# A two-layer hybrid model block in float32 on one core: written first steps, one-shape scores among a projection's matmuls, a second place for two weights, and partition swaps on ACT

## The chip, the core and the metric

The kernel runs on one core of a Trainium2 chip. The core has a matrix engine (TensorE, in the profile PE for matmuls and PEld for weight loads), a vector engine (DVE), a scalar engine (ACT), GpSimd (POOL) and a queue engine (SP) from which most transfers are issued. The metric is the device time of one execution in microseconds (us), as the median of several runs.

## The reference, cut to what matters

Two layers over 256 tokens of width 1024. Each layer has a mixer and a gated feed-forward part, and each of these is preceded by a normalization that is scaled and shifted by a conditioning vector c. Layer 0's mixer is a gated linear recurrence in chunks; layer 1's is attention with three branches (compressed blocks, selected blocks, window).

```python
c_act = silu(c)
mods = einsum('bd,lde->lbe', c_act, ada_w) + ada_b      # shift, scale, gate of 4 sublayers
# layer 0
h = rms_norm(x, gain) * (1 + scale) + shift
q, f, i, g = split(h @ w_in)          # 4 x 1024 columns
q = silu(q); log_f = log_sigmoid(f); k = 1 - exp(log_f)
# per head, with G = cumsum(log_f):
attn[t, s] = sum_d q[t, d] * k[s, d] * exp(G[t, d] - G[s, d])     # s <= t
o = rms_norm(attn @ i + state terms) * silu(g)
x = x + gate * (o @ w_out);  x = x + gate * swiglu(h')
# layer 1
k_cmp, v_cmp, k_sel, v_sel, k_win, v_win = split(modulate(x, kv_norm) @ w_kv)
kc = rms_norm(silu(blocks(k_cmp) @ w1) @ w2)       # compressed keys, values alike
q = rms_norm(h @ w_q); k_sel, k_win = rope(rms_norm(.)); q_rope = rope(q)
o = g0 * attend(q, kc, vc) + g1 * attend(q_rope, k_sel, v_sel) + g2 * attend(q_rope, k_win, v_win)
x = x + gate * (o @ w_out);  x = x + gate * swiglu(h'')
```

## The kernel before, in words

Activations lie transposed: width on 128 partitions in eight chunks, 256 tokens along the free dimension. Products are made nearly float32 in three matmuls (`mm3`, L484): each weight and each activation is split into a rounded part and a residual, `wh`, `wl` and `hh`, `hl`. ACT makes `wh` by a cast (L309) and DVE makes `wl` by a subtraction (L310), two halves of 128x1024 for each weight chunk.

**The stream of weights.** All weights come as chunks of 128x2048 float32 (1 MB) in one list, SCHED, whose order is written by hand through ORDER. `issue` (L284) starts transfers from SP into a ring of RAW = 4 buffers; `process` (L293) takes the next chunk and either splits it ("lin"), holds it as it is ("raw": the compression's four weight chunks w1, of which each step c0 and c1 uses two), or uses it for conditioning. A held chunk keeps its buffer until `release_raw` (L336); `issue` lets the list run at most RAW chunks past the oldest held one. Conditioning chunks are reduced on DVE (`ada`, L354: two reductions over 1024 columns and small operations) or multiplied on PE (`ada_pe`, L376) with a 32-column stationary operand.

**Order of the instructions.** A program step is written in sequence, and the tile framework then places the instructions of each engine by their readiness and priority, so a later step's matmuls may come ahead of an earlier step's. `issue_after` ties an instruction behind a given one; `after` (L435) adds an order without a wait.

**Start.** `build` loads crow (c as a row), x in two halves, the columns and the first ring. It spreads c over the partitions (`crep`, L249, two matmuls and Silu on ACT). `first_stat` (L553) squares x (two quarters on ACT, two on DVE), adds the quarters in three DVE operations of 512 columns (L567), and sums over partitions and the remaining two chunks with two fp32 matmuls (`ms`, L569, each recorded as two passes). Then comes the inverse root: Ln and Exp on ACT, and four DVE operations (L574 to L578).

**Recurrent layer** (`hgrn`, L674). For each of the eight input chunks k: one conditioning chunk on DVE, `full_chunk` (L599: t on DVE, hh on ACT, hl on DVE), and 48 matmuls with the q and f columns. Then ORDER["hgrn"] is walked: D makes the decays X of two pairs of heads (ACT exponentials, DVE products; a pool of 14 X buffers), i and g are projections of 48 matmuls, S and T are the scores of a pair of heads, V the values. A pair has four calls of `head_scores` (L862): 24 small matmuls into psl, and the "upper" scores into psu: one matmul with 64 columns (L880) and two with 32 (L884). T differs from S in that projection g2 is cut into eight pieces (`gate_steps`, L724) and tied between the calls.

**Attention layer** (`nsa`, L1019). It projects keys and values (kv), makes hq (the queries' normalized input, `full_pair` L608) and hk (the values'), then walks ORDER["nsa"]: c compression (two halves), q query projections, G gates, n query norms, s, x, v scores and values, w the value projection, a conditioning. hh and hl of "which 0" share the memory h0; the k and v compression projections read it, and hk is written into it ahead of the compression. `rotate` (L983) makes the rotary embedding; it needs each group of 32 partitions exchanged with its neighbour, and does that with four transfers of 64 KB issued from ACT (L989). It is called for two key tiles and four query tiles.

## Time and profile before

| | |
|---|---|
| runs of the kernel | 749.25, 749.32, 747.56 us; median 749.25 |
| the profiled execution | span 749.9 us from its first to its last instruction; no other time of it is given |
| PE busy | 719.1 us (96%) |
| DVE busy | 587.9 us (78%) |
| ACT busy | 410.8 us (55%) |
| moved from HBM | 170.48 MB, 229 GB/s over the span |

A row of a timeline holds the start, the duration, the engine, the line of the kernel, the operation, the tiles written and read, their shapes and the count; in brackets stand the idle time of the engine before it and what ended that. A group row holds the count, the busy time of the group and the mean of one in ns, then the idle time before them. PE's busy time includes waiting inside the pipeline, so the distance between starts of matmuls says more than the busy share. A matmul in float32 is recorded as two passes.

### The profile page before, as it was taken

Reading aid. Unit: us, or ns where it says so; the run is one execution under the profiler, and the core shown is the slowest. Engines: PE = TensorE matmul, PEld = TensorE weight load, DVE = VectorE, ACT = ScalarE, POOL = GpSimd, SP = SyncE. Lnnn points to the kernel's source line nnn. Section 1 sums busy time; section 2 is a strip of 40 time slices with the busy share of each in tenths; the row PEclk is TensorE's granted clock in tenths of the full one; section 3 lists DMA queues with packets and bytes.
Section 4 is the critical chain, followed back from the end, with each engine's and each line's share of the span. In section 5 each row is a group of like instructions: output and inputs, shape, how many; then the busy total and the mean of one; then the engine's idle time right before and its main releaser. Section 6 shows DMA issues by size and latency. Waiting matters only on the chain.

```text
span 749.9 us, 14669 instructions
## 1 busy us (share of the span) xinstructions
PE 719.1 (96%) x5892; PEld 634.2 (85%) x5892; DVE 587.9 (78%) x1221; ACT 410.8 (55%) x796; POOL 0.4 (0%) x5
## 2 busy tenths in 40 slices
PE   4999998899999999999999789999999999999997
PEld 2999986799999999988897688655799888888886
DVE  6995988479898988898689667777689869776642
ACT  4348868356645544544476443756666665565330
POOL 0000000000000000000000000000000000000000
PEclk9999999999999999999999998999999999999999
DMA  8998737556389797888733834355764555756710
GB/s 343 340 346 343 272 111 276 208 222 225 120 338 385 273 362 272 328 317 319 283 113 96 318 121 141 113 196 198 282 212 181 193 201 214 268 191 225 271 45 21
DMA packets 26566, 174.05 MB, mean 232 GB/s; under 512 B 3201, under 2 KB 4609, under 8 KB 6018
## 3 DMA queue, kind: packets, MB, share of 16 engines
q1 hardware_dynamic: 24912, 170.80, 61.1%
q10 hardware_dynamic: 1586, 2.32, 1.1%
q8 instruction: 46, 0.75, 0.4%
q14 instruction: 22, 0.18, 0.1%
HBM read 170.48 MB, written 1.05 MB: 229 GB/s over the span
## 4 chain that ended last, share of the span: by engine, by line
PE 86%; DVE 7%; DMA 3%; ACT 2%; issue 1%; ACTq 0%; DVEq 0%
PE ffo L498 11%; PE ff L486 6%; PE ff L488 6%; PE ff L487 6%; PE ffo L499 6%; PE ff L498 5%; PE ff L499 2%; PE adapsss L387 2%; PE po L1321 2%; DMA usq<-huq 2%; PE ptt L1304 2%; DVE wl L310 2%; PE s L1264 1%; PE q L487 1%; PE hg_i L781 1%; PE hg_g L486 1%
## 5 line engine op out<-in xcount | busy, mean ns | idle before, releaser
L309 ACT CAST wh<-raw 128x1024 fp32r<-128x1024 f32 x201 | 208.9, 1048 | 170.3 <-PE ffo L498 47.7
L310 DVE TENSOR_TENSOR wl<-raw,wh 128x1024 fp32r<-128x1024 f32 x201 | 244.2, 1221 | 58.5 <-ACT wh L309 57.8
L498 PE MATMUL ffo<-g,wh 128*128 128x512 f32 x352 | 123.5, 394 | 0.0
L499 PE MATMUL ffo<-g,wl 128*128 128x256 f32 x352 | 99.1, 282 | 0.0
L486 PE MATMUL ff<-hh,wh 128*128 128x256 f32 (+1 forms) x352 | 99.0, 282 | 0.0
L487 PE MATMUL ff<-hl,wh 128*128 128x256 f32 (+1 forms) x352 | 98.9, 282 | 0.0
L488 PE MATMUL ff<-hh,wl 128*128 128x256 f32 (+1 forms) x352 | 98.7, 281 | 0.0
L498 PEld LDWEIGHTS ffo<-g,wh 128*128 128x128 f32 x352 | 66.2, 188 | 15.3
L361 DVE CUSTOM_DVE_ANT_0 junk<-raw,crep 128x1024 f32<-128x1024 f32 x64 | 78.1, 1220 | 0.5
L488 PEld LDWEIGHTS ff<-hh,wl 128*128 128x128 f32 x352 | 66.5, 189 | 0.0
L487 PEld LDWEIGHTS ff<-hl,wh 128*128 128x128 f32 x352 | 66.3, 189 | 0.2
L486 PEld LDWEIGHTS ff<-hh,wh 128*128 128x128 f32 x352 | 66.2, 188 | 0.0
L499 PEld LDWEIGHTS ffo<-g,wl 128*128 128x128 f32 x352 | 66.1, 188 | 0.0
L498 PE MATMUL ff<-h,wh 128*128 128x512 f32 x152 | 54.2, 395 | 0.0
L499 PE MATMUL ff<-h,wl 128*128 128x256 f32 x152 | 42.6, 280 | 0.0
L498 PEld LDWEIGHTS ff<-h,wh 128*128 128x128 f32 x152 | 28.7, 189 | 6.8 <-DVE h L605 0.2
L431 ACT ACTIVATE Pt<-Pt,nm 128x128 f32<-128x128 f32 x64 | 28.1, 442 | 8.9 <-DVE nm L1273 8.8
L656 DVE SCALAR_TENSOR_TENSOR x<-ffo,mod,x 128x256 f32<-128x256 f32 x32 | 15.4, 482 | 18.4 <-PE ffo L499 18.1
L499 PEld LDWEIGHTS ff<-h,wl 128*128 128x128 f32 x152 | 28.6, 188 | 0.0
L481 ACT CAST g<-fg 128x256 fp32r<-128x256 f32 x44 | 17.8, 404 | 17.4 <-DVE fg L950 16.5
L488 PE MATMUL nq<-hh,wl 128*128 128x256 f32 x64 | 20.1, 314 | 3.6 <-DVE wl L310 3.6
L1269 DVE CUSTOM_DVE_ANT_0 Pt<-s,cst 128x128 f32<-128x128 f32 (+1 forms) x64 | 19.1, 352 | 2.8 <-PE s L1264 2.7
(453 smaller groups left out, 1741.4 us busy)
## 6 DMA issues: line engine op xcount, KB each, us to landing
raw<-in_w SPq DMA_DIRECT2D x160, 1024.0 KB, 5.3
x<-in_x SPq DMA_DIRECT2D x2, 512.0 KB, 4.8
usq<-huq ACTq DMA_DIRECT2D x16, 64.0 KB, 2.1
out<-x SPq DMA_DIRECT2D x8, 128.0 KB, 1.9
cst<-in_cst ACTq DMA_DIRECT2D x1, 558.0 KB, 6.9
usk<-huk ACTq DMA_DIRECT2D x8, 64.0 KB, 2.8
raw<-in_w SPq DMA_DIRECT2D x1, 512.0 KB
rselr<-in_rsel SPq DMA_DIRECT2D x1, 256.0 KB, 2.7
```

The source lines that it names most:

```text
L309: nc.scalar.copy(wh, u)
L310: nc.vector.tensor_tensor(wl, u, wh.bitcast(F32), op=ALU.subtract)
L361: nc.vector.tensor_tensor_reduce(out=junk, in0=t[:, h * D:(h + 1) * D], in1=self.crep, scale=1.0, scalar=0.0, op0=ALU.mult, op1=ALU.add, a ...
L431: r = nc.scalar.activation(out, in_, func, **kw)
L481: self.nc.scalar.copy(hi, v)
L486: mm(ps, lhsT=wh, rhs=hh, start=first, stop=False)
L487: mm(ps, lhsT=wh, rhs=hl, start=False, stop=False)
L488: return mm(ps, lhsT=wl, rhs=hh, start=False, stop=last)
L498: mm(ps, lhsT=w[k][0], rhs=b, start=k == 0, stop=False)
L499: mm(ps[:, 0], lhsT=w[k][1], rhs=b[:, 0], start=False, stop=k == n - 1)
L656: nc.vector.scalar_tensor_tensor(xn[:, m], p, gate[:, m:m + 1], xn[:, m], op0=ALU.mult, op1=ALU.add)
L1269: nc.vector.tensor_tensor_reduce(out=Pt[half][:, br, o:o + n], in0=ps[half][:, br], in1=cs[:, S - n:], scale=1.0, scalar=-3e38, op0=ALU.ad ...
```

## The change

1. **First steps.** `startup` replaces the steps of `build` and most of `first_stat`. Each half of x gets its own run: a square on ACT, a square on DVE, two additions on DVE, one `ms` matmul. `chain` adds an order without a wait to the instructions of ACT, of DVE and of PE, in which the Silu of c stands between the squares. For layer 0 the small steps of a conditioning chunk go to ACT, with a product `gb` made once. The inverse root has two operations on DVE (L574 to L578 had four), with a Square and a product on ACT, and the first conditioning chunk is processed ahead of them. Chunks 1 to 7 use `first_chunk`: x times the normalizer on DVE, scale and shift on ACT, a copy on ACT, a subtraction on DVE.
2. **Filler.** 14 matmuls of zeros (bf16, 256 columns) stand between the mean and the first projection.
3. **Scores.** The 64-column matmul of the upper scores becomes two of 32 columns. Projection g1 is cut into four pieces that are tied between the calls of S0; g2 is cut into eight over S2 and S3 as before; conditioning chunks of layer 0's gate and of sublayer 1 move to other places in the list ("hada").
4. **A second home.** The chunks w1 2 and 3 (LATE) no longer use the ring. `load_late` puts them into the memory of h0 after the k projections; hk is made after the compression (step K behind c1); `issue` counts held buffers; and chunks up to nq0 are processed right after `load_late`.
5. **Swaps.** The four transfers of `rotate` become four copies on ACT.

```diff
 ORDER = {
-        "D0 i0 g0 S1 i1 S0 V0 D1 g1 i2 i3 T2 T3 V1"
+        "D0 i0 g0 S1 i1 g1/4 S0 c1 V0 D1 i2 i3 g2/8 S2 S3 V1 g3"
-    "hada": [1, 1, 3, 4, 6, 6, 6, 7, 7, 7, 8, 8],
+    "hada": [1, 1, 2, 2, 3, 3, 4, 4, 7, 7, 8, 8],
-        "c0 q0 c1 G q1 n0 x0 s0 w0 q2 s1 q3 w1 s2 v0 v1 ...
+        "c0 q0 c1 K G q1 n0 x0 s0 w0 q2 s1 q3 w1 s2 v0 v1 ...
+LATE = [("raw", "w1", 2), ("raw", "w1", 3)]
     def issue(self, n):
-        n = min(n, len(SCHED), min(self.held, default=n) + RAW)
+        n = min(n, len(SCHED))
+        free = RAW - sum(i < self.n_proc for i in self.held)
+        ring = [i for i in range(self.n_proc, n) if SCHED[i] not in LATE]
+        n = min(n, ring[free]) if len(ring) > free else n
         while self.n_dma < n:
+            if SCHED[self.n_dma] in LATE:
+                self.n_dma += 1
+                continue
...
+    def load_late(self):
+        t = self.hp.tile([P, KD, 2, 258], F32R, tag="h0", name="w1late").rearrange("p k e s -> p (k e s)").bitcast(F32)
+        for kind in range(2):
+            n = SCHED.index(LATE[kind])
+            d = t[:, kind * CH:(kind + 1) * CH]
+            self.nc.sync.dma_start(d, self.a["w"][n])
+            self.rawready[("w1", 2 + kind)] = (None, d)
...
-        if kind == "ada_ss":
+        if kind == "ada_ss" and l == 0:
+            nc.scalar.activation(A[:, i:i + 1], m[:, c1:c1 + 1], AF.Identity, scale=gain[:, i:i + 1],
+                                 bias=self.gb[:, i:i + 1])
+            nc.scalar.activation(m[:, i:i + 1], m[:, i:i + 1], AF.Identity, bias=bias[:, i:i + 1])
...
+    def startup(self, crow):
+        v.memset(mean, 1.0 / D)
...
+        pe = [nc.tensor.matmul(p, lhsT=self.ones[0:1, :], rhs=crow[0:1, 512 * h:512 * h + 512], start=True, stop=True)
+              for h, p in enumerate(pc)]
+        on_act, on_dve = [], []
+        for h in range(2):
+            c, d = 4 * h, 4 * h + 2
+            on_act.append(nc.scalar.activation(sq[:, c:d], x[:, c:d], AF.Square))
+            on_act.append(self.act(self.crep[:, 512 * h:512 * h + 512], pc[h], AF.Silu))
+            on_dve += [v.tensor_tensor(sq[:, d:d + 2], x[:, d:d + 2], x[:, d:d + 2], op=ALU.mult),
+                       v.tensor_tensor(sq[:, c:d], sq[:, c:d], sq[:, d:d + 2], op=ALU.add),
+                       v.tensor_tensor(sq[:, c], sq[:, c], sq[:, c + 1], op=ALU.add)]
+            pe.append(nc.tensor.matmul(ps, lhsT=mean, rhs=sq[:, c], start=h == 0, stop=h == 1))
+        on_act.append(self.act(cc, self.col("c"), AF.Silu))
+        self.chain(*on_act)
+        self.chain(*pe)
+        self.warm = pe[-1]
+        on_dve.append(v.tensor_scalar_add(self.b1, self.cols[:, lo:lo + 112], 1.0))
+        on_dve.append(v.tensor_tensor(self.gb, self.b1[:, 8:16], self.col(self.gain(0)), op=ALU.mult))
+        on_dve.append(v.tensor_copy(self.c32, cc[:, :, None].to_broadcast([P, 8, 32])))
+        self.chain(*on_dve)
     def first_stat(self):
         self.act(y, ps, AF.Ln, bias=self.eps)
         self.act(y, y, AF.Exp, scale=-0.5)
-        nc.vector.tensor_tensor(t, y, y, op=ALU.mult)
+        nc.scalar.activation(t, y, AF.Square)
+        nc.scalar.mul(w, y, -0.5)
+        self.process()
         nc.vector.scalar_tensor_tensor(t, ps, EPS, t, op0=ALU.add, op1=ALU.mult)
-        nc.vector.tensor_scalar(t, t, -0.5, 1.5, op0=ALU.mult, op1=ALU.add)
-        nc.vector.tensor_tensor(self.rstd, t, y, op=ALU.mult)
+        nc.vector.scalar_tensor_tensor(self.rstd, t, -3.0, w, op0=ALU.add, op1=ALU.mult)
+    def first_chunk(self, hh, hl, m, A, sh, pool):
+        r = nc.vector.tensor_tensor(xr, self.x[:, m], self.rstd, op=ALU.mult)
+        self.after(r, self.hl_prev)
+        nc.scalar.activation(t, xr, AF.Identity, scale=A[:, m:m + 1], bias=sh[:, m:m + 1])
+        self.last_hh = nc.scalar.copy(hh[:, m, :256], t)
+        self.hl_prev = nc.vector.tensor_tensor(hl[:, m, :256], t, hh[:, m, :256].bitcast(F32), op=ALU.subtract)
...
+            for _ in range(14):
+                z = nc.tensor.matmul(pq[0][:, 0], lhsT=self.zero, rhs=self.zero[:, :1].to_broadcast([P, S]), start=True, stop=True)
+                self.after(z, self.warm)
+                self.warm = z
...
-        nc.tensor.matmul(u[0:64, 64:128], lhsT=X[6][:, h, base:base + 64],
-                         rhs=X[6][:, h, base + 64:base + 128], start=True, stop=True,
-                         tile_position=(0, 0))
+        for j in (0, 32):
+            nc.tensor.matmul(u[j:j + 32, 64:128], lhsT=X[6][:, h, base + j:base + j + 32],
+                             rhs=X[6][:, h, base + 64:base + 128], start=True, stop=True,
+                             tile_position=(0, j))
...
-            nc.scalar.dma_start(us[d:d + 32], u[e:e + 32])
+            nc.scalar.copy(us[d:d + 32], u[e:e + 32])
...
+                self.load_late()
+                while self.n_proc <= SCHED.index(("lin", "nq", 0)):
+                    self.process()
...
-                hk = self.full_pair(0, "kv", xr, s2, KACT)
...
+                    elif t[0] == "K":
+                        hk.append(self.full_pair(0, "kv", xr, s2, KACT))
+                        early.close()
+                        self.s3 = self.late.enter_context(self.tc.tile_pool(name="nsp", bufs=PTS))
```

More of the change, by code (lines that the diff above doesn't have):

```diff
@@ L245, in build @@
         self.issue(RAW)
-        self.crep = self.cp.tile([P, D], F32, name="crep")
-        for h in range(2):
-            ps = self.m_tile([P, 512], f"crep{h}")
-            nc.tensor.matmul(ps, lhsT=self.ones[0:1, :], rhs=crow[0:1, 512 * h:512 * h + 512], start=True, stop=True)
-            self.act(self.crep[:, 512 * h:512 * h + 512], ps, AF.Silu)
-        lo = COLS["ada_b0"][0]
-        self.b1 = self.cp.tile([P, 112], F32, name="b1")
-        nc.vector.tensor_scalar_add(self.b1, self.cols[:, lo:lo + 112], 1.0)
-        cc = self.cp.tile([P, 8], F32, name="cc")
-        self.act(cc, self.col("c"), AF.Silu)
-        self.c32 = self.cp.tile([P, 8, 32], F32, name="c32")
-        nc.vector.tensor_copy(self.c32, cc[:, :, None].to_broadcast([P, 8, 32]))
+        self.startup(crow)
         self.hgrn()
@@ L551, in stat, with chain @@
             self.ssum = nsum
+    def chain(self, *steps):
+        for p, n in zip(steps, steps[1:]):
+            self.after(n, p)
+    def startup(self, crow):
+        nc = self.nc
+        x, v = self.x, nc.vector
+        sq = self.hp.tile([P, KD * 258], F32, tag="hh1", name="sqs")[:, :KD * S].rearrange("p (k s) -> p k s", k=KD)
+        mean = self.tp.tile([P, 2, P], F32, tag="dg", bufs=1, name="mean")[:, 0]
+        v.memset(mean, 1.0 / D)
+        self.crep = self.cp.tile([P, D], F32, name="crep")
+        cc = self.cp.tile([P, 8], F32, name="cc")
+        self.c32 = self.cp.tile([P, 8, 32], F32, name="c32")
+        pc = [self.m_tile([P, 512], f"crep{h}") for h in range(2)]
+        ps = self.m_tile([P, S], "ms")
+        pe = [nc.tensor.matmul(p, lhsT=self.ones[0:1, :], rhs=crow[0:1, 512 * h:512 * h + 512], start=True, stop=True)
[13 more added lines that the diff above has]
+        self.warm = pe[-1]
+        lo = COLS["ada_b0"][0]
+        self.b1 = self.cp.tile([P, 112], F32, name="b1")
+        on_dve.append(v.tensor_scalar_add(self.b1, self.cols[:, lo:lo + 112], 1.0))
+        self.gb = self.cp.tile([P, 8], F32, name="gb")
+        on_dve.append(v.tensor_tensor(self.gb, self.b1[:, 8:16], self.col(self.gain(0)), op=ALU.mult))
+        on_dve.append(v.tensor_copy(self.c32, cc[:, :, None].to_broadcast([P, 8, 32])))
+        self.chain(*on_dve)
+        self.ms = ps
@@ L553, in first_stat @@
     def first_stat(self):
         nc = self.nc
-        sq = self.hp.tile([P, KD * 258], F32, tag="hh1", name="sqs")[:, :KD * S].rearrange("p (k s) -> p k s", k=KD)
-        mean = self.tp.tile([P, 2, P], F32, tag="dg", bufs=1, name="mean")[:, 0]
-        nc.vector.memset(mean, 1.0 / D)
-        ps = self.m_tile([P, S], "ms")
-        for e in range(4):
-            d, x = sq[:, 2 * e:2 * e + 2], self.x[:, 2 * e:2 * e + 2]
-            if e < 2:
-                nc.scalar.activation(d, x, AF.Square)
-            else:
-                nc.vector.tensor_tensor(d, x, x, op=ALU.mult)
@@ L566, in first_stat @@
-        for e in (1, 2, 3):
-            nc.vector.tensor_tensor(sq[:, 0:2], sq[:, 0:2], sq[:, 2 * e:2 * e + 2], op=ALU.add)
-        for k in range(2):
-            nc.tensor.matmul(ps, lhsT=mean, rhs=sq[:, k], start=k == 0, stop=k == 1)
+        ps = self.ms
         y = self.tp.tile([P, S], F32, tag="sq", name="fy")
         t = self.tp.tile([P, S], F32, tag="sq", name="ft")
+        w = self.tp.tile([P, S], F32, tag="ssum", name="fw")
         self.act(y, ps, AF.Ln, bias=self.eps)
         self.act(y, y, AF.Exp, scale=-0.5)
-        nc.vector.tensor_tensor(t, y, y, op=ALU.mult)
+        nc.scalar.activation(t, y, AF.Square)
@@ L755, in hgrn @@
                 elif t[0] == "g":
[L756 removed]
+                    if t[2:]:
+                        between = gate_steps(n, int(t[3:]))
+                    elif n < 2:
+                        nc.scalar.copy(graw[:, n], gate_in(n))
+                    else:
+                        gin[n] = None
+                elif t[0] == "c":
+                    nc.scalar.copy(graw[:, n], gin[n])
                 elif t[0] == "V":
```

134 lines of the change are left out of this document (74 added, 60 removed).

## The prediction

> **What bounds the kernel now.** I read the page's head and chain first, then a table of busy time by stretch, then the timelines of three stretches.
>
> ```profile
> span 749.9 us, 14669 instructions
> PE 719.1 (96%) x5892; PEld 634.2 (85%) x5892; DVE 587.9 (78%) x1221; ACT 410.8 (55%) x796; POOL 0.4 (0%) x5
> ...
> PE 86%; DVE 7%; DMA 3%; ACT 2%; issue 1%; ACTq 0%; DVEq 0%
> ```
> ```profile
> 0.00:18.70 18.70, 7.68 (x15) 3.90 (x16) 11.46 (x27) 9.11 (x13) 0.20 (x4) 1.00 0.89 344
> 65.50:100.00 34.50, 34.44 (x551) 31.12 (x553) 28.60 (x62) 30.45 (x49) 0.00 (x0) 1.00 0.63 238
> ...
> 128.00:161.00 33.00, 30.65 (x553) 26.57 (x553) 18.62 (x42) 15.17 (x39) 0.00 (x0) 0.95 0.65 256
> 161.00:372.00 211.00, 210.28 (x1588) 201.29 (x1587) 185.18 (x331) 108.92 (x167) 0.00 (x0) 1.00 0.76 287
> 396.00:475.00 79.00, 69.24 (x490) 60.74 (x488) 59.98 (x154) 37.95 (x92) 0.00 (x0) 0.94 0.46 160
> ```
>
> The columns of the table are stretch, length, then busy PE, weight loads, DVE, ACT, POOL, granted clock, DMA share, GB/s. TensorE carries 86% of the chain. In the first feed-forward part (161 to 372) it is busy 210.28 of 211 us, and nothing in the diff touches that arithmetic, so a gain can only come from where TensorE waits or runs slowly: before 18.7 us (7.68 busy of 18.7), in the recurrent part (65.5 to 161), and at the entry of the attention (396 to 475: 69.24 busy of 79 and a mean clock of 0.94). The change edits exactly these three. I sum them one by one. The span, 749.9 us, is the only time shown of the profiled execution; the runs have a median of 749.25 (747.56 to 749.32), so I take the gains off 749.25. About 0.3% (2.2 us) is what a measurement of this kernel can tell from no change.
>
> **First steps.** Timeline of the first 24 us, and the answer for the tile x:
>
> ```profile
> 7.20 1.28 DVE L565 TENSOR_TENSOR sqs<-x 128x512 f32<-128x512 f32 x2
> 8.52 2.14 DVE L567 TENSOR_TENSOR sqs<-sqs 128x512 f32<-128x512 f32 x3
> 10.58 1.22 DVE L361 CUSTOM_DVE_ANT_0 junk<-raw,crep 128x1024 f32<-128x1024 f32 x1
> 10.71 2.07 PE L569 MATMUL ms<-sqs,mean 128*128 128x256 f32 x4 [4.05 <-DVE sqs L567]
> 14.25 0.42 DVE L575 SCALAR_TENSOR_TENSOR ft<-ms,ft 128x256 f32<-128x256 f32 x1
> 15.49 0.48 DVE L603 SCALAR_TENSOR_TENSOR t<-x,modA,rstd 128x256 f32<-128x256 f32 x1
> 15.90 2.35 DVE L310 TENSOR_TENSOR wl<-raw,wh 128x1024 fp32r<-128x1024 f32 x2
> 16.02 0.51 ACT L604 ACTIVATE h<-t,mod 128x256 fp32r<-128x256 f32 x1 [0.39 <-DVE t L603]
> 18.70 0.58 PE L487 MATMUL q<-h,wh 128*128 128x256 f32 x1 [0.26 <-DVE h L605]
> 21.43 0.41 PE L486 MATMUL q<-h,wh 128*128 128x256 f32 x1
> 21.64 0.41 PE L487 MATMUL q<-h,wh 128*128 128x256 f32 x1
> 23.23 0.28 PE L486 MATMUL f<-h,wh 128*128 128x256 f32 x1
> 23.35 0.28 PE L487 MATMUL f<-h,wh 128*128 128x256 f32 x1
> ```
> ```profile
> L222 SPq DMA_DIRECT2D x<-in_x x2: 378/400/422, 0.7 to 1.2; - x2
> DMA to landing us min/median/max: 4.3/4.8/5.3
> ```
>
> DVE is the engine of the start. The halves of x land at 0.7+4.3 = 5.0 and 1.2+5.3 = 6.5 us, but DVE squares at 7.20, and the mean's four passes begin only at 10.71, after the third addition. The written order lets DVE take each half as it lands: a square (0.64), a wide addition (0.71) and a narrow one (0.42, the narrow row) are 1.77 us, so the halves end at 6.8 and 8.6, and only two of the four passes (1.04) stand behind the last: the mean is there at 9.65, against 10.71+2.07 = 12.78. Then DVE has three small operations (together about 0.6, an estimate from the narrow row) and the first two conditioning reductions (2.5), to about 11.8; they, not the mean, are late next. The normalizer now takes two DVE steps (0.84) instead of four, t 0.48, two weight residuals 2.35, hl 0.48 (t's form): 16.0 us. Against 18.70 that is 2.7 earlier; with hl ahead of the second residual it would be 3.9. I take 3.0. Later input chunks lose their two small conditioning steps on DVE to ACT, which is idle enough (9.11 of 18.7); DVE only has to keep up with 48 matmuls of 0.12.
>
> The second term is the clock. The profile's clock row says 1.00 from the start, but matmuls start 0.21 apart at 21.43 and 0.12 apart at 23.23: the first 4 us of the dense stream run at little over half speed, which costs 4.0 x (1 - 0.12/0.21) = 1.7. The 14 fillers take 14 x 0.21 = 2.9 us behind the mean, in time in which TensorE has nothing else, so they cost nothing unless the first inputs arrive before 12.6. They can win between 0 and 1.7; I take 1.2, because 1 to 3 us of idleness still lie between the last filler and the first real matmul. Start: **-4.2** (from -2.7 to -5.6).
>
> The Trainium skill ("TensorE: Matmul & The Clock Gate", Part 1) says that the gate opens only after a free-running window of about 3.4 us of sustained activity; by it, 2.9 us of fillers with the mean's passes just ahead may or may not fill a window, and the sum would be 1.2 us smaller where they don't. The trace agrees on the size: 18.70 to between 21.64 and 23.23.
>
> **Recurrent part.** TensorE's timeline and its groups by shape:
>
> ```profile
> 67.91 1.93 PE L387 MATMUL adapsg<-raw,c 128*32 128x256 f32 x32
> ```
> ```profile
> 128.73 0.53 PE L875 MATMUL psl<-X 128*32 128x16 f32 x40
> 129.20 0.33 PE L880 MATMUL psu<-s 128*64 128x64 f32 x2
> 129.45 0.26 PE L884 MATMUL psu<-X 128*32 128x32 f32 x4
> 129.64 0.38 PE L486 MATMUL hg_g<-h,wh 128*128 128x256 f32 x1
> ```
> ```profile
> L880 PE MATMUL psu<-s 128*64 128x64 f32 x32 | 5.5, 251 | 3.4 <-issue 1.8 <-DVE s L825 1.6
> ```
>
> One head's upper scores take 129.20 to 129.64, 0.44 us, for six small instructions, because the 64-column shape stands between two runs of 32-column shapes. Cut into 32 columns, the whole head has one shape; conditioning matmuls of that shape cost 1.93/32 = 0.06 at 256 columns, so four of 64 cost about 0.06 together, and the four others about 0.04: 0.34 saved. There are 16 such heads. For S1 and S0 I count nothing: ACT is busy 30.45 of 34.5 from 65.5 to 100, making their decays, and what TensorE saves it then waits. For S2 and S3 (128 to 161, ACT 15.17 and DVE 18.62 of 33) TensorE is the bound: 8 x 0.34 = 2.7. Against it: projection g1, 48 matmuls of 0.12 = 5.7 us, is now spread inside S0 and no longer free to fill the time until the second decays are done; the row shows 1.6 us of waiting for them already. S0 ends later, its X buffers come free later: I add 1.2. The 1.8 us put down to issue in the same row I leave as it is. Conditioning matmuls moved earlier count the same wherever they fill. Recurrent part: **-1.5** (from -4.2 to +4.7).
>
> The Trainium skill ("TensorEngine Tiling (Array Packing)", Key Properties) says that a change of tiling mode drains the array; that speaks for the single shape and against spreading, since four cuts in g1 add eight switches. No row separates the two; the issue starts 0.44 apart agree with a price for each switch.
>
> **Entry of the attention.** Timeline and ACT's groups:
>
> ```profile
> 416.09 0.39 PE L486 MATMUL gates<-hh,wh 128*128 128x256 f32 x1 [0.78 <-ACT wh L309]
> 417.35 0.38 PE L488 MATMUL gates<-hh,wl 128*128 128x256 f32 x1 [0.76 <-DVE wl L310]
> 419.75 2.00 ACT L309 CAST wh<-raw 128x1024 fp32r<-128x1024 f32 x2 [2.67 <-DMA raw<-in_w]
> 419.97 0.75 DVE L993 SCALAR_TENSOR_TENSOR usq<-usq,cols,cst 128x512 f32<-128x512 f32 x1 [2.68 <-DMA usq<-huq]
> 420.85 0.39 PE L486 MATMUL nq<-hh,wh 128*128 128x256 f32 x1 [1.33 <-ACT wh L309]
> 424.32 0.39 PE L488 MATMUL nq<-hh,wl 128*128 128x256 f32 x1 [2.26 <-DVE wl L310]
> 445.63 0.75 DVE L993 SCALAR_TENSOR_TENSOR usq<-usq,cols,cst 128x512 f32<-128x512 f32 x1 [3.36 <-DMA usq<-huq]
> 447.79 0.60 PE L1228 MATMUL cs<-KC,QN 128*128 128x32 f32 x4 [2.34 <-DVE QN L1017]
> ```
> ```profile
> L309 ACT CAST wh<-raw 128x1024 fp32r<-128x1024 f32 x12 | 12.4, 1045 | 17.8 <-PE nq L487 12.8 <-DMA raw<-in_w 4.9
> L481 ACT CAST h<-t 128x256 fp32r<-128x256 f32 x8 | 3.1, 404 | 0.1
> ...
> L616 ACT ACTIVATE t<-xr,modkv,modAkv 128x256 f32<-128x256 f32 x4 | 2.4, 599 | 1.2 <-DVE h L482 1.2
> L977 ACT COPY huq<-nq 128x512 f32<-128x512 f32 x4 | 2.3, 580 | 6.2 <-PE nq L488 6.2
> ```
>
> Two causes show. First, four compression weights lie in the ring of four buffers until the compression has read them, so ng and nq1 are fetched only then: TensorE waits 0.78+0.76+1.33+2.26 = 5.1. With the last two loaded into h0's memory, both follow nq0 into the ring while the compression's weights are still held. The new loads wait on SP for the last reader of h0, and raw loads behind them in the queue wait too; that reader, the k projections, runs ahead of the compression, so I cost this at nothing; if SP stood there until the compression ends, the 5.1 would stay. Second, DVE stands 2.68 and 3.36 us for swap DMAs with weight residuals queued behind; TensorE's share is 2.34. The mean clock, 0.94 over 79 us, is another 4.7 us, lost right after such waits. Recoverable: 5.1+2.3+4.7 = 12.1.
>
> What comes instead: step K (hk) needs h0, hence the end of the compression. Its ACT work, 4 x 0.60 + 8 x 0.40 = 5.6 us, formerly beside the compression, now stands before the value projection. Its cover is gates and nq1 on TensorE, 72 x 0.12 = 8.6; with two weight casts (2.1) ACT needs 7.7, which just fits; without the cover it costs 5.6. I charge 1.5. The swaps become 24 ACT copies; the nearest row is 0.58 for 512 columns: 13.9 us more on an engine busy 37.95 of 79. They fit, but each set of four holds ACT for 2.3 us with casts queued behind. I charge 2.6. Entry: 12.1 - 1.5 - 2.6 = **-8.0** (from -12.1 to 0).
>
> Sum: 749.25 - 4.2 - 1.5 - 8.0 = 735.55, say **735.6**.
>
> **Rivals.** *All of it*: the start gives 5.6, the middle 4.2 (all 16 heads, 5.4, less 1.2), the entry 12.1: 727.4. For it: three waits share one cause. Against: a freed stretch rarely stays free.
>
> *Second decays late*: S0, stretched by g1's 5.7 us, holds its X buffers so long that TensorE waits 5.7 for S2 and loses 0.05 of 33 us more clock (1.7), less the 2.7: middle +4.7, total 741.8. For it: the 1.6 of waiting; against: S1 frees half the buffers first.
>
> *Entry gains nothing*: hk becomes what the value projection waits for, ACT being in order; 749.25 - 5.7 = 743.6.
>
> *The chains don't order what they say*: they add no waits, and if the first instructions keep their places and the fillers open nothing, the start is 0: 739.8.
>
> *Second decays late and entry nothing, together*: 749.25 - 4.2 + 4.7 = 749.8, no change.
>
> *Slower*: the copies stand in front of weight casts in ACT's in-order queue, so every one of the 13.9 us lies on the path and nothing is recovered at the entry: -4.2 - 1.5 + 13.9, 757.5. It decides once over 7.9 us of copies are on the path. For it: casts wait 17.8 us for buffers in this stretch, so each starts late already; against: ACT is idle half the time there.
>
> **How the numbers follow.** Forecast 0.58 (its own range 731 to 740); all 0.12; decays 0.08; entry nothing 0.06; chains 0.04: faster, 0.88. Both together: same, 0.05. Slower 0.07. The range, 726 to 745.5, runs from "all" to "entry nothing", each with the 1.8 us spread of the runs, and leaves out the last two cases.
>
> **What would show it.** First dense matmul at 15 to 16 us and starts 0.12 apart within 2 us of it; the last f matmul some 4 us earlier; no 64-column psu group and about 0.1 us for a head's upper scores; no DMA on usq or usk; gates and nq waiting under 1 us for casts; granted clock above 0.97 from 396 to 475. I am wrong if v waits for hk by more than 3 us, if psu waits for decays by over 4, or if ACT copies end TensorE's waits.

## The result, and the profile after

| | runs | median us | ratio to before, 95% interval |
|---|---|---|---|
| kernel before | 4 (747.56 to 749.32) | 749.01 | |
| changed kernel | 4 (737.16 to 740.48) | 738.88 | 0.9866 [0.9842, 0.9891] |
| changed kernel, a second time | 6 (736.93 to 741.48) | 739.68 | 0.9881 [0.9846, 0.9917] |

The change makes the kernel 10.1 us faster (8.2 to 11.8 by the first interval). The forecast was 735.6, a gain of 13.7. The changed kernel's profiled execution has a span of 737.4 us and a time of 739.74, and the spans of its other runs lie 1.8 to 2.1 us under their times; the next table of stages goes by spans.

The head of the changed kernel's page and its chain:

```profile
span 737.4 us, 14753 instructions
PE 715.3 (97%) x5938; PEld 630.7 (86%) x5938; DVE 581.8 (79%) x1205; ACT 433.7 (59%) x845; POOL 0.4 (0%) x5
...
PE 85%; DVE 7%; ACT 6%; issue 1%; DMA 1%; DVEq 0%; ACTq 0%
```

Its table of busy time by stretch (stretch, length, busy PE, weight loads, DVE, ACT, POOL, clock, DMA share, GB/s):

```profile
0.00:15.15 15.15, 9.14 (x23) 4.28 (x23) 8.52 (x22) 8.48 (x16) 0.21 (x4) 1.00 0.87 345
65.50:100.00 34.50, 31.56 (x521) 24.80 (x513) 29.05 (x66) 26.81 (x44) 0.00 (x0) 0.95 0.75 285
128.00:161.00 33.00, 28.41 (x513) 24.81 (x511) 17.74 (x45) 13.96 (x38) 0.00 (x0) 0.95 0.57 226
161.00:372.00 211.00, 210.60 (x1590) 201.70 (x1590) 184.96 (x330) 108.19 (x165) 0.15 (x1) 1.00 0.76 287
395.00:465.00 70.00, 67.40 (x506) 57.73 (x508) 60.88 (x160) 52.24 (x120) 0.00 (x0) 0.98 0.44 164
```

The start and the entry of the attention are fuller than before; the entry has 2.6 us without TensorE in 70, where it had 9.8 in 79, and a clock of 0.98 after 0.94. The two stretches of the recurrent part are not fuller but emptier: 2.9 us without TensorE from 65.5 to 100, where there were 0.1, and 4.6 from 128 to 161, where there were 2.4. The clock in them is 0.95 and 0.95, where it was 1.00 and 0.95.

Where the time came from is read off the first matmul of three steps: the values' projection (hg_i, when the dense start is over), the recurrent layer's output (hgo) and the attention's output (nso). In the timeline of the kernel before:

```profile
65.45 0.28 PE L781 MATMUL hg_i<-wh,h 128*128 128x256 f32 x1
156.82 0.28 PE L486 MATMUL hgo<-hh,wh 128*128 128x256 f32 x1
535.48 0.39 PE L486 MATMUL nso<-h,wh 128*128 128x256 f32 x1
```

and of the changed kernel:

```profile
62.94 0.28 PE L852 MATMUL hg_i<-wh,h 128*128 128x256 f32 x1
155.09 0.28 PE L504 MATMUL hgo<-hh,wh 128*128 128x256 f32 x1
522.68 0.39 PE L504 MATMUL nso<-h,wh 128*128 128x256 f32 x1
```

| stage | before | after | difference | forecast |
|---|---|---|---|---|
| start, up to hg_i | 65.45 | 62.94 | -2.5 | -4.2 |
| recurrent part, hg_i to hgo | 91.37 | 92.15 | +0.8 | -1.5 |
| hgo to nso (feed-forward, attention) | 378.66 | 367.59 | -11.1 | -8.0 |
| nso to the end | 214.4 | 214.7 | +0.3 | 0 |
| sum | 749.9 | 737.4 | -12.5 | -13.7 |

Two of the three terms missed in one direction and one in the other. One profile stands on each side, though, and the split between the stages moves from one execution to the next. From hg_i to hgo, four profiles with the changed kernel's list up to there (this one, its repeat, and the first two runs below, which edit only later steps) have 92.15, 94.05, 90.97 and 95.77 us. The run of the kernel before with 16 tiny matmuls more at its start, last of the experiments, has 95.98 where the table has 91.37, and 371.99 from hgo to nso where it has 378.66. So a row of these two stages is good to some 5 to 7 us, and their sum is firmer than either.

The start explains itself in TensorE's and DVE's timelines of the changed kernel:

```profile
9.10 1.22 PE L597 MATMUL ms<-sqs,mean 128*128 128x256 f32 x2 [0.63 <-DVE sqs L596]
10.12 3.16 PE L743 MATMUL q<-zero 128*128 128x256 bf16 x14
15.15 0.74 PE L504 MATMUL q<-h,wh 128*128 128x256 f32 x4 [1.87 <-ACT h L652]
16.54 0.41 PE L505 MATMUL q<-h,wh 128*128 128x256 f32 x1
19.95 0.28 PE L506 MATMUL q<-h,wl 128*128 128x256 f32 x1
```
```profile
9.58 1.23 DVE L370 CUSTOM_DVE_ANT_0 junk<-raw,crep 128x1024 f32<-128x1024 f32 x1
11.77 0.42 DVE L623 SCALAR_TENSOR_TENSOR ft<-ms,ft 128x256 f32<-128x256 f32 x1 [0.95 <-ACT ft L620]
12.11 1.22 DVE L370 CUSTOM_DVE_ANT_0 junk<-raw,crep 128x1024 f32<-128x1024 f32 x1
```

DVE stands still for 0.95 us for a Square on ACT, and the second conditioning reduction follows only after it. TensorE idles 1.87 us behind the fillers, and from 16.54 to 19.95 its matmuls start 0.21 apart again.

In the recurrent part TensorE stands in the midst of the smallest matmuls and waits for nothing that the profile shows. Timeline of the changed kernel, behind it the line of the DMA queues that both the window from 129 to 133 us and that from 135 to 139 give (queue, packets, MB, share), and the page's line of the same queue for the whole span:

```profile
130.35 0.27 PE L940 MATMUL psl<-q,X 128*32 128x32 f32 x8
...
132.04 0.46 PE L946 MATMUL psl<-X 128*32 128x16 f32 x33 [1.37 <-issue]
...
138.23 0.44 PE L946 MATMUL psl<-X 128*32 128x16 f32 x32 [2.46 <-issue]
```
```profile
q8 instruction: 1, 0.02, 1.5%
```
```profile
q8 instruction: 46, 0.75, 0.4%
```

Each of the two windows holds one transfer on the queue "instruction", of 16 KB. The trace has their starts at 129.61 and 135.81 us; TensorE goes on at 132.04 and 138.23, 2.4 us behind the start both times. In the kernel before, the wait for issue that the prediction left alone stands behind such a transfer too (133.08). The whole execution has 46 of these transfers for 5938 matmuls, 129 matmuls each; by this count they are TensorE's own program, and in the scores a block of it lasts two heads (a head has 48 small matmuls, 8 of the upper scores and 6 of projection g2). This became the theory for the recurrent part: TensorE runs out of instructions. The Trainium skill ("Runtime: NRT & Kernel Launch", Instruction fetch mechanics) says that the program is refilled in blocks of 16 KiB, 256 instructions, and that crossing a block is mostly hidden. The trace agrees on the block (a matmul and its weight load are two instructions), and not on the hiding: 1.37 and 2.46 us are waited.

### The profile page after: what moved, and what is told of

Same layout as the page of the kernel before. It is cut to its first block, busy times and chain, and to the rows that moved or that the text cites. A ratio compares the mean times of both kernels' runs of the same rounds, so it can differ in the third digit from the quotient of the medians.

```text
span 737.4 us, 14753 instructions
## 1 busy us (share of the span) xinstructions
PE 715.3 (97%) x5938; PEld 630.7 (86%) x5938; DVE 581.8 (79%) x1205; ACT 433.7 (59%) x845; POOL 0.4 (0%) x5
## 4 chain that ended last, share of the span: by engine, by line
PE 85%; DVE 7%; ACT 6%; issue 1%; DMA 1%; DVEq 0%; ACTq 0%
PE ffo L516 11%; PE ff L506 6%; PE ff L505 6%; PE ff L504 6%; PE ffo L517 6%; PE ff L516 5%; PE po L1399 3%; PE ff L517 2%; PE adapsss L404 2%; PE ptt L1382 2%; PE s L1342 2%; DVE wl L308 1%; PE nso L504 1%; PE q L505 1%; PE q L506 1%
## 5 line engine op out<-in xcount | busy, mean ns | idle before, releaser
L504 PE MATMUL hg_g<-h,wh 128*128 128x256 f32 x64 | 20.0, 313 | 0.0
```

What stands on the lines that cost most here:

```text
L504: mm(ps, lhsT=wh, rhs=hh, start=first, stop=False)
```

## The experiments

The theories as they stood: the entry gains by the ring and by the swaps, in the sizes forecast; the fillers by an open clock gate; the scores by their one shape, less what TensorE's own program takes back. Times are compared by their ratio to the kernel before, which ran beside them on the same chip (its medians were 748.42, 747.87 and 749.10 for the three groups of runs). Stages are compared by one profile each.

**The swaps back on DMA.**

```diff
-            nc.scalar.copy(us[d:d + 32], u[e:e + 32])
+            nc.scalar.dma_start(us[d:d + 32], u[e:e + 32])
```

> The changed kernel with the partition swaps of the rotary step as transfers again, all else kept. Two causes were named for the waits at the attention's entry, the ring and the swap transfers. If both matter (my theory), the transfers bring back a DVE wait of 2 to 3 us for usq, TensorE waits of about 2.3 us and a slow clock after them: about 4.5 us more than the changed kernel's 738.9, 743.4, ratio to before 0.9925. If the ring alone made the gain, the time stays within 1 us of 738.9.

Measured: 742.5 us (740.14 to 744.99), ratio 0.9924 [0.9898, 0.9950]. The step from hgo to nso took 370.97 us, 3.4 more than in the changed kernel. DVE waits 2.46 us for the keys' swap, TensorE 2.12 and 1.51 us behind it, and from 406.0 to 412.7 the clock is 0.50, so the waits come back as expected, at the keys instead of the queries. ACT's rows show why the copies were cheap; first the timeline of ACT in this run, then ACT's group of the queries' copies in the changed kernel from 390 to 465 us:

```profile
406.27 2.44 ACTq L1061 DMA_DIRECT2D usq<-huq  x4
408.75 2.94 ACT L307 CAST wh<-raw 128x1024 fp32r<-128x1024 f32 x3 [2.02 <-DMA usq<-huq]
```
```profile
L1061 ACT COPY usq<-huq 32x512 f32<-32x512 f32 x16 | 9.9, 617 | 0.2
```

Four DMA issues hold ACT's queue for 2.44 us, and the weight casts queue behind them just as they queue behind four copies of 0.617 (2.47). The copies take no more of ACT than the issues did, and the landing is saved. The forecast charged the copies and forgot the issues.

**The old ring and the old place of hk.** LATE is emptied, `issue` counts as in the kernel before, the early processing goes, step K stands ahead of the compression again; the ACT swaps stay. Ring and place of hk change together, so this run doesn't part them.

```diff
-        "c0 q0 c1 K G q1 n0 x0 s0 w0 q2 s1 q3 w1 s2 v0 v1 n1 s3 s4 a v2 v3 a a a x1 s5 a a s6 v4 v5 s7 a v6 a a "
+        "K c0 q0 c1 G q1 n0 x0 s0 w0 q2 s1 q3 w1 s2 v0 v1 n1 s3 s4 a v2 v3 a a a x1 s5 a a s6 v4 v5 s7 a v6 a a "
-LATE = [("raw", "w1", 2), ("raw", "w1", 3)]
+LATE = []
...
-                self.load_late()
-                while self.n_proc <= SCHED.index(("lin", "nq", 0)):
-                    self.process()
```

> The changed kernel with all four compression weights in the ring again and hk made ahead of the compression, swaps still on ACT. If both causes matter, TensorE waits about 5 us for gates and nq weights again and loses some clock: about 6 us more than 738.9, 745, ratio 0.9945. If the swaps alone made the gain, within 1 us of 738.9. If the two gains need each other, it is as slow as the kernel before less the start, about 746.5, and so is the run with transfers.

Measured: 749.16 us (745.70 to 752.52), ratio 1.0014 [0.9993, 1.0035]. This is more than was expected. The profile is of its slowest execution (752.52). In it, 9.0 us more lie between hgo and nso (376.59 against 367.59), and 3.6 in the recurrent part, which no edit touches. TensorE's timeline at the entry:

```profile
410.22 0.79 PE L1082 MATMUL hb<-hry,rsel 128*128 128x256 f32 x2 [3.63 <-ACT hry L496]
426.43 0.39 PE L501 MATMUL gates<-hh,wh 128*128 128x256 f32 x1 [1.09 <-ACT wh L304]
428.01 0.39 PE L503 MATMUL gates<-hh,wl 128*128 128x256 f32 x1 [1.07 <-DVE wl L305]
```

The waits of the gates for casts and residuals are back, and the key norm on ACT, which the copies and probably hk's work now precede, makes TensorE wait 3.63 us. Against the kernel before (378.66) the copies alone leave 2.1 us of gain in this stretch, and none against that kernel's run with the shift (371.99). By the medians, all the other edits together gain nothing without this one (ratio 1.0014).

**No fillers, and 30 of them** (the same line with 30).

```diff
-            for _ in range(14):
+            for _ in range(0):
```

> The changed kernel without the 14 filler matmuls. In the changed kernel's profile the last filler ends near 13 us, the first real matmul comes at 15.15, and the dense stream from 16.54 runs 0.21 apart until 19.95: the fillers seem to win nothing because TensorE idles after them. My theory: no change, within 0.7 us of 738.9, dense stream still at 16.5 and full speed by 20 us. Rival, as the prediction had it: the fillers win 1.2 us, so 740.1, and full speed comes later than 20 us.

> The changed kernel with 30 fillers in place of 14, to bridge the idle time up to the first real matmul. My theory: the gate stays open, matmuls from the first dense one on start 0.12 apart, and 0.8 to 1.5 us are won: about 737.7. Rival: 16 more fillers at 0.21 end at 16.5 us, push the first real matmul back by about 1.3 us and win nothing: 739 to 740.

Measured: without fillers 740.43 us (739.09 to 742.24), ratio 0.9896 [0.9874, 0.9919]; with 30, 735.68 us (735.57 to 736.18), ratio 0.9834 [0.9813, 0.9855]. Step hg_i begins at 63.27 without, 62.94 with 14 and 62.45 with 30. So by these profiles the 14 are worth 0.3 us and 16 more another 0.5; but seven profiles with the changed kernel's own first steps lie between 62.46 and 63.55, so neither is told from nothing. That the median without fillers is 1.6 us higher, as the rival had it, is not their doing at the start: its profile has 2.7 us more from hg_i to hgo. With 30 the fillers reach the first projection and the gate stays open, but TensorE's timeline then has a new wait, and DVE is full (second fence, stretch 12 to 23):

```profile
13.78 1.05 PE L743 MATMUL q<-zero 128*128 128x256 bf16 x8
15.00 0.74 PE L504 MATMUL q<-h,wh 128*128 128x256 f32 x4 [0.18 <-ACT h L652]
22.31 0.74 PE L504 MATMUL q<-h,wh 128*128 128x256 f32 x4 [0.88 <-ACT h L664]
```
```profile
12.00:23.00 11.00, 9.75 (x75) 8.61 (x74) 10.17 (x17) 6.22 (x11) 0.00 (x0) 1.00 0.98 382
```

DVE is busy 10.17 of 11 us; the second chunk is late whatever TensorE's clock. And most of the gain of the 30 lies where no filler stands: from hg_i to hgo the profiles have 88.65 us, after 92.15 with 14 and 94.85 with none. That pointed to the place in TensorE's list, which the fillers shift.

**The same shift without a bridge.** 16 matmuls of 16 columns ahead of the first mean matmul, where TensorE waits for x:

```diff
+            if h == 0:
+                for _ in range(16):
+                    pe.append(nc.tensor.matmul(ps[:, :16], lhsT=self.zero, rhs=self.zero[:, :16], start=True, stop=True))
             pe.append(nc.tensor.matmul(ps, lhsT=mean, rhs=sq[:, c], start=h == 0, stop=h == 1))
```

> The changed kernel with 16 more matmuls of 16 columns of zeros ahead of the first mean matmul, in time in which TensorE waits for data anyway: they shift every later TensorE instruction by 16 places in its list, as the run with 30 fillers did, but they do not bridge the idle time ahead of the first projection. Theory of the instruction supply: the waits put down to issue depend on where the list is cut into blocks of 16 KB and move or shrink as they did with 30 fillers, and most of that run's gain in the recurrent part comes without any bridge: 736 to 737, ratio 0.983 to 0.985, with starts 0.21 apart until about 20 us as in the changed kernel. Rival, the bridge: only fillers that reach the first projection gain; nothing changes here, ratio 0.9866 within 0.002, and the waits for issue are where the changed kernel has them.

Measured: 735.31 us (734.50 to 736.15), ratio 0.9840 [0.9812, 0.9867], as the theory of the supply has it and against the rival; all four runs lie under the lowest of the changed kernel's ten. Step hg_i begins at 62.94, as in the changed kernel; hg_i to hgo takes 88.63 us. Timeline of this run, then the stretch from 133 to 146 us of the changed kernel and of this one:

```profile
128.58 0.27 PE L943 MATMUL psl<-q,X 128*32 128x32 f32 x8
...
130.18 0.27 PE L943 MATMUL psl<-q,X 128*32 128x32 f32 x8
...
135.13 0.27 PE L943 MATMUL psl<-q,X 128*32 128x32 f32 x8 [1.33 <-issue]
...
139.40 0.23 PE L943 MATMUL psl<-q,X 128*32 128x32 f32 x3 [0.62 <-issue]
```
```profile
133.00:146.00 13.00, 10.54 (x271) 9.55 (x270) 4.54 (x11) 3.66 (x8) 0.00 (x0) 0.87 0.32 132
```
```profile
133.00:146.00 13.00, 11.04 (x237) 8.79 (x238) 5.81 (x12) 5.92 (x19) 0.00 (x0) 1.00 0.41 150
```

The waits for issue fall from 1.37 + 2.46 to 1.33 + 0.62, 1.9 us. The clock falls to half behind the wait of 2.46 us only: 0.87 over 13 us is 1.7 us lost, and here it is 1.00. Together 3.6, against 92.15 - 88.63 = 3.5 measured. (A profile each; the 30 fillers, with the same shift of 16, have 88.65.)

**One of the two upper-score matmuls wide again**, with as many instructions as the changed kernel; first at its place in the list, later with the shift of 16:

```diff
-        for j in (0, 32):
-            nc.tensor.matmul(u[j:j + 32, 64:128], lhsT=X[6][:, h, base + j:base + j + 32],
-                             rhs=X[6][:, h, base + 64:base + 128], start=True, stop=True,
-                             tile_position=(0, j))
+        nc.tensor.matmul(u[0:32, 64:128], lhsT=X[6][:, h, base:base + 32],
+                         rhs=X[6][:, h, base + 64:base + 128], start=True, stop=True,
+                         tile_position=(0, 0))
+        nc.tensor.matmul(u[0:64, 64:128], lhsT=X[6][:, h, base:base + 64],
+                         rhs=X[6][:, h, base + 64:base + 128], start=True, stop=True,
+                         tile_position=(0, 0))
```

> The changed kernel, in which one of the two 32-column matmuls of each head's upper scores is made 64 columns wide again; the number of instructions and their places stay the same, and nothing is left out. My forecast's reason: the mix of two shapes costs TensorE time at every head. By the changed kernel's profile a head's upper scores take 0.24 to 0.29 us against 0.44 before, so 16 x 0.17 = 2.7 us if all of it lay on the path, and 1.4 us if only the heads of the second half do: 738.9 + 1.4 to 2.7 = 740.3 to 741.6, ratio to the kernel before 0.988 to 0.990, and the upper scores back at about 0.44 us. Rival: the stretches with scores are set by the decays and by TensorE's waiting for its own program, so that the shape is worth nothing: 738.9, ratio 0.9866, with the group still at 0.44.

> The changed kernel with both edits that ran alone before: 16 more tiny matmuls early, and one of the two upper-score matmuls of each head 64 columns wide. With the wide shape alone the time stayed (738.5), with the shift alone it was 735.3. Theory: with the list's blocks at the worse places the supply hid what the one shape saves; with the blocks at the better places the shape's saving shows, 16 x 0.17 = 2.7 us at most: 737 to 738, ratio 0.986 to 0.988. Rival: the shape is worth nothing here, 735.3, ratio 0.984.

Measured: at the old place 738.52 us (737.49 to 742.18), ratio 0.9888 [0.9861, 0.9915], the same as the changed kernel; with the shift 738.76 (737.03 to 740.01), ratio 0.9867 [0.9833, 0.9900], against 735.3 and 735.9 (ratios 0.9840 and 0.9828) for the narrow shape with a shift of 16 or 32. Timeline of the first of these runs:

```profile
132.45 0.27 PE L940 MATMUL psl<-q,X 128*32 128x32 f32 x8
...
134.43 0.27 PE L940 MATMUL psl<-q,X 128*32 128x32 f32 x8
```

A head takes 134.43 - 132.45 = 1.98 us here and 130.18 - 128.58 = 1.60 with one shape, and the wide scores have no wait for issue over 0.2 us between 122 and 146, with or without the shift. So one shape does save 0.38 us a head, but TensorE then uses up a block of its program in 3.3 us instead of 4.1, and at the changed kernel's place in the list the waits take the whole saving back. With a shift, 2.0 to 2.9 us of it remain by the ratios. The same pair speaks against early matmuls helping by themselves: where the shape is wide, no gain clear of the noise shows (738.5 and 738.8). The pace alone doesn't decide, though: in the kernel before, 60 matmuls a head in 1.89 us use up a block in some 4.0 us (an estimate), and it waits 1.81 us all the same.

**The changed kernel again, and a shift of 32** (the loop above to 32).

> The changed kernel once more, beside the three that follow on the same chip, so that they can be compared with it without the kernel before in between. Both theories: 738.9, ratio 0.9866 within 0.002; stretch from the last f matmul to the output projection 92.3 us, waits for issue in the score stretches at the same places.

> The changed kernel with 32 instead of 16 more tiny matmuls early. From the last f matmul to the output projection the profiles have 95.0 us with 14 matmuls fewer, 92.3 with the changed kernel's list, 88.8 with 16 more of either kind. Theory of the instruction supply: only the place of the blocks' edges counts, so the next 16 places change the stretch again by 1 us or more in either direction (87 to 96 us; time 733 to 742), and the waits for issue lie elsewhere than with 16. Rival: early matmuls help by themselves, by whatever means; then 32 are as good as 16, 735.3 within 1 us, with the same 88.8 and the same waits.

Measured: again 739.68 us (first table); with 32, 735.93 us (735.11 to 738.83), ratio 0.9828 [0.9793, 0.9864]. The time with 32 lies within both expectations, so this run doesn't tell them apart. Its profile is of its slowest execution (738.83) and has a wait for issue of 2.33 us that its other runs, at 735.1 to 736.4, may lack. The repeat of the changed kernel has a wait of 2.38 us in an earlier score stretch, where the first profile has 0.41:

```profile
89.89 0.34 PE L946 MATMUL psl<-X 128*32 128x16 f32 x10 [2.38 <-issue]
```

So the place is not all: the same list waits more or less from one execution to the next, which fits the spread of 4.6 us in its runs, against 1.7 with the shift of 16. But the place does say where a wait can come. The fourteen traces have 23 waits for issue of more than 1 us in the recurrent part. Counted in matmuls from the start of the program, they come after 731, 1115, 1497 or 1498, and 1625 or 1626, whatever the kernel: three, three and one block of 128 apart. Each ends 2.2 to 2.6 us after the start of an instruction transfer. The wait of 0.41 in the first profile and that of 2.38 in the repeat both come after 731 matmuls. What a shift changes is which of the scores lie at such an edge.

**The old order of the recurrent part**, with one shape.

```diff
-        "D0 i0 g0 S1 i1 g1/4 S0 c1 V0 D1 i2 i3 g2/8 S2 S3 V1 g3"
+        "D0 i0 g0 S1 i1 S0 V0 D1 g1 i2 i3 g2/8 S2 S3 V1 g3"
-    "hada": [1, 1, 2, 2, 3, 3, 4, 4, 7, 7, 8, 8],
+    "hada": [1, 1, 3, 4, 6, 6, 6, 7, 7, 7, 8, 8],
```

> The changed kernel with the old order in the recurrent part: g1 in one piece behind S0, g2 in eight pieces over S2 and S3, and the conditioning chunks at their old places; the one shape of the scores and all else stay. My forecast charged the new order 1.2 us for later second decays: by it, 738.9 - 1.2 = 737.7, ratio 0.985, with shorter waits of the first scores of S2 for decays. Rival: spreading g1 and the conditioning fill gaps of S0 that the old order leaves open, about 2 us: 741, ratio 0.989. Under 1 us either way would mean that TensorE's sum of work sets the stretch and the order does not.

Measured: 740.80 us (739.51 to 742.73), ratio 0.9915 [0.9891, 0.9940]. The new order doesn't cost the 1.2 us charged; by the medians it gains 1.9, by the ratios 2.5 to 3.7, but the interval touches that of the changed kernel, and the old order's score stretches have waits for issue too (3.93 and 1.83 us). What the order is worth by itself stays open. One thing this run does settle: it has no wait of the first scores for X, while every profile with the new order has 2.3 us of them, with the wide shape as well.

**Both late projections spread**, to thin out the small instructions.

```diff
-        "D0 i0 g0 S1 i1 g1/4 S0 c1 V0 D1 i2 i3 g2/8 S2 S3 V1 g3"
+        "D0 i0 g0 S1 i1 g1/4 S0 c1 V0 D1 i2 i3 g2/4 S2 g3/4 S3 V1"
```

> The changed kernel with another order in the second half of the recurrent part: projection g2 is cut into four pieces tied between the calls of S2 and projection g3 into four between those of S3 (the changed kernel cuts g2 into eight over both and runs g3 behind). Twice as many large matmuls stand between the small ones, so that TensorE takes its instructions from the list at about half the pace there. Theory of the instruction supply: the waits put down to issue in S2 and S3 (1.55 and 2.64 us in the changed kernel's profile) vanish or fall under 0.5 us each, and the stretch from the last f matmul to the output projection, 92.3 us, becomes 2 to 4 us shorter: 735 to 737, ratio 0.981 to 0.984. Rival: those waits are not of the supply's making and lie at fixed places of the list, or g3's work only moves: no change, ratio 0.9866 within 0.002.

Measured: 743.06 us (740.31 to 747.66), ratio 0.9931 [0.9908, 0.9954]: slower, and the theory's expectation failed. One wait for issue of 2.05 us remained in the second half (and one of 1.67 ahead of it), and g3 no longer stands behind the scores as cover for the output's chain:

```profile
160.83 0.63 PE L985 MATMUL hgt<-cst,o 128*128 128x128 f32 x4 [2.31 <-DVE o L982]
...
164.19 0.80 PE L504 MATMUL hgo<-hh,wh 128*128 128x256 f32 x2 [1.28 <-ACT hh L499]
```
```profile
163.80:170.60 6.80, 6.39 (x28) 6.10 (x29) 3.95 (x6) 2.72 (x5) 0.00 (x0) 0.50 0.00 1
```

The second fence is the busy table behind these waits: the clock is at half for 6.8 us.

**The kernel before with the shift.**

```diff
+        for _ in range(16):
+            nc.tensor.matmul(ps[:, :16], lhsT=self.zero, rhs=self.zero[:, :16], start=True, stop=True)
         for k in range(2):
             nc.tensor.matmul(ps, lhsT=mean, rhs=sq[:, k], start=k == 0, stop=k == 1)
```

> The kernel before with 16 matmuls of 16 columns of zeros ahead of its mean matmuls, where TensorE waits for data; nothing else is changed. If the place of the blocks' edges is a matter of this list as well, the kernel before moves too, by 1 to 4 us in either direction, through its one wait for issue of 2.08 us and the half clock behind it (3.4 us at half speed, 1.7): ratio between 0.995 and 1.003, and that much of the difference between the two kernels is a matter of place and not of the change. Rival: the effect belongs to the new order with scores of one shape: 748.4, ratio 1.000 within 0.0015.

Measured: 746.17 us (744.96 to 751.89), ratio 0.9982 [0.9955, 1.0009]. Seven runs lie at 745.0 to 746.7 and five at 748.4 to 751.9; the kernel before itself has 744.1 to 753.2. Whether the shift helps it can't be told, so how much of the 10.1 us is a matter of places in the list, and not of the change, stays open within some 3 us. Its profile (span 748.3) divides the time otherwise than the first one of the kernel before:

```profile
161.84 0.28 PE L486 MATMUL hgo<-hh,wh 128*128 128x256 f32 x1
533.83 0.39 PE L486 MATMUL nso<-h,wh 128*128 128x256 f32 x1
```

## Why the prediction was right or wrong

**Faster, inside the range, 3.3 us too fast.** The bottleneck was read rightly: the gain came where TensorE waited or ran slowly, and the untouched feed-forward stretch stayed. How the gain divides over the stages is known less well than the sum, so part of the agreement is luck: the recurrent part missed by +2.3 and the entry by -3.1 in the first pair of profiles.

**What the gains were taken off.** In the profiles the gain is 12.5, 1.2 us short of the forecast's 13.7. The rest is the step "so I take the gains off 749.25", with a profile of another execution than the median one. Runs are 1.8 to 2.3 us longer than their spans (a later run of the kernel before: 749.10 with a span of 747.3), so the execution with the span 749.9 belongs to a run of about 752, some 2.5 us above the median. That much of the waits in the profile the median run hadn't got to lose. Some of them were probably at the entry (below).

**Start: -2.5 for -4.2.** Two terms were mis-sized. The dense stream starts at 16.54, not 15.7: DVE's wait for ACT's Square (0.95) and the second reduction behind it were counted as beside each other, and they are in a row; the gain is 2.2, not 3.0. The fillers won 0.3 at most by these profiles, not 1.2. "1 to 3 us of idleness still lie between" was right (1.87): by the clock column the clock is full over the fillers and at half again behind the idleness.

```profile
9.10:13.10 4.00, 4.00 (x16) 2.62 (x16) 3.01 (x7) 1.91 (x6) 0.00 (x0) 1.00 1.01 426
13.20:16.50 3.30, 1.23 (x8) 0.95 (x8) 2.73 (x7) 2.67 (x4) 0.00 (x0) 1.00 1.00 417
16.60:19.90 3.30, 3.30 (x17) 3.30 (x17) 3.30 (x5) 1.23 (x2) 0.00 (x0) 0.50 0.90 293
```

From 13.2 to 16.5 TensorE is busy 1.23 us at full clock, and the next 3.3 us run at 0.50; the trace's clock changes at 13.10, 16.52 and 19.93 us, 3.41 apart. The rule cited ahead of the result, a free-running window of about 3.4 us ("TensorE: Matmul & The Clock Gate" of the Trainium skill, Part 1), fits these edges. The cap that the forecast gave, 1.7, was not reached with 30 fillers either, since DVE is late next.

**Recurrent part: +0.8 for -1.5.** The price of the shape came out right: 0.34 a head forecast, 1.60 against 1.98 us measured where instructions arrive, and 1.60 against 132.65 - 130.76 = 1.89 in the kernel before:

```profile
130.76 0.27 PE L869 MATMUL psl<-q,X 128*32 128x32 f32 x8
132.65 0.27 PE L869 MATMUL psl<-q,X 128*32 128x32 f32 x8
```

That it fits is in part luck: the upper scores themselves fell from 0.44 us to 0.27 (129.00 to 129.27 in the run with the shift of 16), not to 0.1, and 0.14 more came from the 40 matmuls ahead of them, which the forecast didn't count (0.47 us before, 0.33 with one shape). The rule on draining between modes ("TensorEngine Tiling (Array Packing)" of the Trainium skill, Key Properties) goes with a saving of this kind; no run parts a drain from the matmuls' own time. The step that failed is "The 1.8 us put down to issue in the same row I leave as it is". It was TensorE waiting for its program, and it grew: 1.37 + 2.46 in S2 and S3, 4.9 in the whole part. The 1.7 of clock behind it is no growth, since the kernel before lost as much there (0.95 in both tables). The feared waits for the second decays (1.6 before) did not come.

A second step failed: "For S1 and S0 I count nothing", with "Conditioning matmuls moved earlier count the same wherever they fill". TensorE waits 2.3 us for X in the changed kernel's first scores, where the kernel before had no such wait, and then runs at half clock for 3.4 us. The wait comes with the new order and not with the shape, since the run with the old order has none and the wide shape has it too; which move of the order makes it, no run shows.

```profile
86.31 0.22 PE L946 MATMUL psl<-X 128*32 128x16 f32 x5 [1.76 <-DVE X L896]
```
```profile
88.20:91.60 3.40, 3.14 (x34) 3.03 (x24) 3.40 (x11) 2.17 (x3) 0.00 (x0) 0.50 0.52 173
```

Added up as an estimate: 3.1 more for issue (4.9 for 1.8), 0.7 more for decays (2.3 for 1.6) and 1.7 of clock, less 16 x 0.29 for the shape, are +0.9, and +0.8 was measured.

**Entry: -11.1 for -8.0.** Recoverable were 12.1, and by these two profiles nearly all came: what remains over 0.5 us in the changed kernel are two waits.

```profile
398.80 0.62 PE L1076 MATMUL hs<-hsqk,cst 128*32 128x256 f32 x2 [1.00 <-ACT hsqk L1126]
406.21 0.39 PE L504 MATMUL nq<-hh,wh 128*128 128x256 f32 x1 [1.02 <-ACT wh L307]
```

But the 12.1 were read off an execution that was slow here. The kernel before with the shift took 371.99 us for this stretch, 6.7 less: DVE waits 2.0 us for the queries' swaps instead of 6.0, TensorE 0.2 us for QN instead of 2.3, and one stretch of 3.4 us runs at half clock instead of three. Whether the 16 tiny matmuls or chance makes that difference isn't shown. Against that run the entry gained 4.4, so the gain lies between 4.4 and 11.1, and whether the forecast of 8.0 was too low or too high stays open. The charges of 1.5 for hk and 2.6 for the copies look too high on other grounds: the copies cost ACT what the DMA issues cost it (2.47 and 2.44 us for four), and TensorE shows no wait for hk. By the single edits, one profile each, the ring with hk is worth 9.0 and the swaps 3.4. Their sum is over the 11.1 of both, so some of the gain seems to need both edits, but 1.3 us is less than such profiles differ by.

**The signs named.** First matmul at 15 to 16: right (15.15). Starts 0.12 apart 2 us later: wrong, 4.8. Last f 4 us earlier: 2.5. A head's upper scores at 0.1: 0.2 to 0.3. No swap DMAs, clock above 0.97 at the entry: right. Gates and nq under 1 us: 1.02, just missed. None of the three signs of being wrong appeared; the waits that grew, for issue and for the first decays, were watched by none of them.

The fastest version found is the changed kernel with 16 tiny early matmuls (735.3), with that of 30 fillers (735.7) not distinguishable from it.

## What to carry to other kernels

A wait that the profile puts down to "issue" in a run of tiny instructions is a resource, not noise: hold the queue of instruction transfers against it before counting on making those instructions cheaper. A gain that is clear in the medians can't be divided over stages by one profile on each side: here the same instructions took 91.0 to 95.8 us in one stage. Before charging a copy that replaces a DMA, count what the issue cost on the engine that issued it. Fillers that end 1.87 us short of the first real matmul didn't keep the clock up for it here, and those that reached it won little more at the start, because another engine was late right behind.

## What the runs showed of the hardware

TensorE's program comes in transfers of 16 KB, one for 129 matmuls. In runs of matmuls of 16 to 64 columns, a block is used up in 3.3 us, and TensorE stood up to 2.46 us in the midst of them in the changed kernel (3.93 with the old order) and went on 2.2 to 2.6 us after the transfer's start. All these waits lie at steps of 128 matmuls in the list. Why the transfer doesn't start earlier is not shown by any run here. In none of the fourteen traces do two of them start less than 3.2 us apart, which suggests a limit of the supply near what one-shape scores use up, but that is argued only. Adding 16 matmuls that compute nothing made the kernel 3.6 us faster by the medians, 1.9 by the ratios.
